# adaLN terms as VectorE dot products with outputs on partitions; the first scale on TensorE by tile pairs

## The chip, the cores and the metric

The kernel runs on one core of a Trainium2 chip. The metric is the device time of one execution in microseconds (us), the median of several. A core has TensorE (PE in the profile, its weight loads PEld), VectorE (DVE), ScalarE (ACT), GpSimd (POOL) and SyncE (SP, which here only issues transfers); each takes its instructions in the order in which they stand, and 16 DMA engines move the data. Data lies in SBUF or, for matmul results, in PSUM, on 128 partitions.

## The reference

One decoder block for 256 tokens of width 2048, all in fp32. The part that the change touches is the conditioning (adaLN): six vectors of 2048 numbers, each a product of the same vector with 2048 columns of a 2048 x 12288 matrix.

```python
c_act = jax.nn.silu(c)                                   # c: 1 x 2048
mod = (c_act @ w_ada[l] + b_ada[l])[:, None, :]          # 2048 x 12288: 100 MB
sh1, sc1, gt1, sh2, sc2, gt2 = jnp.split(mod, 6, axis=-1)
h = rms_norm(x, g_pre_mix[l]) * (1.0 + sc1) + sh1
z = h @ w_in[l]                                          # 2048 x 8000
...
mix = (g_a * o_a + g_b * o_b) @ w_o[l]                   # two attentions, gated
x = x + gt1 * rms_norm(mix, g_post_mix[l])
h = rms_norm(x, g_pre_ffn[l]) * (1.0 + sc2) + sh2
u = causal_dwconv(h @ w_up[l], conv_w[l], conv_b[l])
y = (jax.nn.silu(u[..., :D_FF]) * u[..., D_FF:]) @ w_down[l]
x = x + gt2 * rms_norm(y, g_post_ffn[l])
```

## The kernel before

Activations are kept transposed: a column of 128 channels stands on the partitions, the 256 tokens along the row. So a scale or shift is needed as one number per partition, in a tile of 128 x 16 (`s1`, `sh1`, `gt1`, `s2`, `sh2`, `gt2`).

Weights come as tiles of 128 x 1024 fp32 (512 KB) through SP's queue. For the large products each tile is split into a rounded high part (L116, ScalarE) and a low part (L117, VectorE), and TensorE multiplies in three terms (L129 to L131; L136 and L138 in the later stages). The adaLN matrix isn't split. Its 192 tiles go one of two ways:
- On TensorE (L234): the conditioning vector, padded to 32 columns (`cpad`), is the stationary operand, and the tile streams through. Four groups of columns use four strips of the array.
- On VectorE (L240 for the first tile, L242 for the others): `acc` gathers tile times the vector's number of that partition. At the end four matmuls with a matrix of ones sum `acc` over the partitions (L247).
Either way the result lies along a row, is copied to `rows` (L249, ScalarE) and turned onto the partitions by matmuls with the identity (L270, L300).

The first scale and shift are made together in six k-groups of 2, 2, 2, 2, 4 and 4 blocks of 128 channels (`early_gen`). `SHARE` sends every second tile of the last three groups to VectorE. While the first projection works on group k (stages z0 to z5, `early_z`), the tiles of group k+1 are issued in between; they lie in four buffers of their own (`raw2`), every second one of group 0 in the weights' ring. The later terms (`cols_gen`: gt1, s2, sh2 from z5 through attention and the output projection, gt2 in the up projection) run wholly on VectorE and share the weights' ring. A generator yields after each tile, and `pump` advances it at a rate per weight tile; a scheduler that keeps a timeline of its own then sets the final order of the instructions on each engine. The transfers stand in SP's queue in that order.

At the start, x is squared on ScalarE (L211), summed over the partitions by 16 matmuls with ones (L213), and the reciprocal root (L215, L216) scales x.

Stages on the trace, in us from the span's start: startup to 24.4, z0 to 56.5, z1 to 91, z2 to 115.5, z3 to 163, z4 to 219.5, z5 and attention to 650, output projection to 755, up projection to 980, the rest to 1503.8.

Of the kernel before, what the change touches and what calls it, by code (L numbers as in the profile page):

```python
# [24 lines left out]
SHARE = [99, 99, 99, 2, 2, 2]  # L25
# [18 lines left out]
def block_kernel(ctx: ExitStack, tc: tile.TileContext, a, out: bass.AP):  # L44
# [136 lines left out]
    ones = const.tile([P, P], F32, name="ones")  # L181
    pool.memset(ones, 1.0)
# [16 lines left out]
    cth = const.tile([P, KC], F32, name="cth")  # L199
# [7 lines left out]

    ps_ss = bank("tp")
    for k in range(0, KC, 2):
        sq = xp.tile([P, 512], F32, tag="sq", bufs=2, name="sq").rearrange("p (a b) -> p a b", a=2)  # L210
        act.activation(sq, xT[:, k:k + 2, :], AF.Square)  # L211
        for i in range(2):
            pe.matmul(ps_ss[:, :T], ones, sq[:, i, :], start=(k + i == 0), stop=(k + i == KC - 1))  # L213
# [5 lines left out]
    def ada_gen(src, width, rows, col, on_pe, share=10**9, spread=False):  # L219


        nj = KC // src.shape[0]
        w = 4 * width
        n = src.shape[0]
        acc = None
        ps = bank(on_pe) if on_pe else None
        for t in range(n):
            raw = load_bg(src[t], nj * w, spread and t % 2 == 1)
            for i in range(nj):
                j = t * nj + i  # L230
                if on_pe and t % share != share - 1:
                    for g in range(4):
                        o = i * w + g * width
                        pe.matmul(ps[32 * g:32 * g + 32, :width], cpad[:, j, :], raw[:, o:o + width],  # L234
                                  start=(j == 0), stop=(j == KC - 1 and share > n))
                    continue
                r = raw[:, i * w:i * w + w]
                if acc is None:
                    acc = const.tile([P, WT], F32, tag="acc", bufs=1, name="acc")
                    dve.tensor_scalar(acc[:, :w], r, csil[:, j:j + 1], None, op0=ALU.mult)  # L240
                else:
                    dve.scalar_tensor_tensor(acc[:, :w], r, csil[:, j:j + 1], acc[:, :w], op0=ALU.mult, op1=ALU.add)  # L242
            yield
# [12 lines left out]

    def early_gen(kg, k0, s):

        w = s * 64
        with ExitStack() as order:  # L260
            if kg:
                order.enter_context(tc.issue_after(split_ins[1].ins))
# [654 lines left out]
```

## Time and profile before

| | |
|---|---|
| time, median of 3 runs | 1502.75 us (1501.55 to 1503.86) |
| the profiled execution's own time | 1505.71 us |
| its span, first to last instruction | 1503.8 us |
| mean granted clock of TensorE | 0.988 |
| TensorE busy | 1452.7 us (97%) |
| VectorE busy | 1083.8 us (72%) |
| ScalarE busy | 775.6 us (52%) |
| GpSimd busy | 260.9 us (17%) |
| HBM read | 351.11 MB, 236 GB/s over the span |

The profile is one execution, some 0.2% longer than the median of the runs. An engine's busy time is a sum over stages that have different limits, so it says little of any one. A busy TensorE isn't TensorE at its peak: matmul ends are modelled, and what a run of small matmuls costs is better read from how far apart its neighbours start.

### The profile page before, as it was taken

The numbers are of one execution on the slowest core, as the hardware profiler recorded it, in microseconds if no ns is written. First come the engines' busy times: TensorE is split into PE (matmuls) and PEld (weight loads), VectorE is DVE, ScalarE is ACT, GpSimd is POOL, SyncE is SP. The second block draws the span as 40 slices with busy tenths as digits, with TensorE's granted clock in tenths as the row PEclk, the third lists the DMA queues.
The fourth block names the chain that finished last, engine by engine and source line by source line (L and its number), as shares of the span: only waits on it lengthen the run. The fifth ranks groups of instructions, "written<-read, shape, count | busy, mean of one in ns | idle before, by whom it ended". The sixth has DMA issues, their size and how long they took to land.

```text
span 1503.8 us, 24728 instructions
## 1 busy us (share of the span) xinstructions
PE 1452.7 (97%) x9506; PEld 1278.0 (85%) x9506; DVE 1083.8 (72%) x1488; ACT 775.6 (52%) x1223; POOL 260.9 (17%) x191
## 2 busy tenths in 40 slices
PE   7999999889999999999899989999999999999997
PEld 6988899789899998978788878888888888888886
DVE  3579868978887969767788777877767776444443
ACT  4534435545554655755655445655555555434442
POOL 0034315922413425300000000100000000000000
PEclk9999999999999999999899999999999999999999
DMA  9888868588687867659477777765555557555552
GB/s 373 312 313 323 311 233 266 180 272 271 201 298 235 301 228 259 202 201 388 178 243 251 239 253 266 251 209 190 187 190 189 189 190 242 193 195 190 191 193 99
DMA packets 101525, 356.96 MB, mean 237 GB/s; under 512 B 11760, under 2 KB 12208, under 8 KB 100896
## 3 DMA queue, kind: packets, MB, share of 16 engines
q1 hardware_dynamic: 99936, 350.82, 68.4%
q0 software_dynamic: 1472, 4.58, 1.2%
q8 instruction: 74, 1.21, 0.3%
q14 instruction: 43, 0.35, 0.1%
HBM read 351.11 MB, written 4.24 MB: 236 GB/s over the span
## 4 chain that ended last, share of the span: by engine, by line
PE 38%; DMA 10%; DVE 5%; ACT 1%; issue 1%; SPq 0%; DVEq 0%; ACTq 0%
PE bk_mm L136 8%; PE bk_sc L136 6%; DMA raw<-in_w_ada_dram 6%; PE bk_mm L138 4%; PE bk_sc L138 3%; PE bk_mm L144 3%; PE bk_sc L144 3%; PE bk_sc L146 3%; PE bk_mm L146 3%; PE bk_mm L145 3%; PE bk_sc L145 3%; DMA raw<-in_w_up_dram 2%; DVE acc L242 2%; DMA raw<-in_w_o_dram 2%; DVE wlo L117 2%
## 5 line engine op out<-in xcount | busy, mean ns | idle before, releaser
L117 DVE TENSOR_TENSOR wlo<-raw,whi 128x1024 fp32r<-128x1024 f32 (+3 forms) x472 | 594.3, 1266 | 282.8 <-ACT whi L116 280.7
L116 ACT CAST whi<-raw 128x1024 fp32r<-128x1024 f32 (+3 forms) x472 | 478.3, 1021 | 504.8 <-PE bk_mm L130 91.2
L129 PE MATMUL bk_mm<-h,whi 128*128 128x256 f32 x976 | 284.3, 292 | 0.5 <-DVE pair L376 0.5
L131 PE MATMUL bk_mm<-h,wlo 128*128 128x256 f32 x976 | 279.3, 287 | 0.0
L130 PE MATMUL bk_mm<-h,whi 128*128 128x256 f32 x976 | 279.1, 286 | 0.0
L136 PE MATMUL bk_mm<-h,whi 128*128 128x512 f32 x848 | 266.6, 396 | 1.2 <-ACT whi L116 1.2
L242 DVE SCALAR_TENSOR_TENSOR acc<-raw,csil,acc 128x1024 f32<-128x1024 f32 (+1 forms) x141 | 192.1, 1362 | 57.9 <-DMA raw<-in_w_ada_dram 57.3
L129 PEld LDWEIGHTS bk_mm<-h,whi 128*128 128x128 f32 x976 | 187.9, 193 | 16.0 <-issue 11.6
L138 PEld LDWEIGHTS bk_mm<-h,wlo 128*128 128x128 f32 x848 | 158.7, 188 | 44.8 <-DVE wlo L117 7.8
L130 PEld LDWEIGHTS bk_mm<-h,whi 128*128 128x128 f32 x976 | 188.3, 193 | 1.7 <-issue 1.7
L131 PEld LDWEIGHTS bk_mm<-h,wlo 128*128 128x128 f32 x976 | 187.8, 193 | 1.4 <-issue 1.3
L136 PE MATMUL bk_sc<-h,whi 128*128 128x512 f32 x560 | 177.1, 398 | 0.0
L138 PE MATMUL bk_mm<-h,wlo 128*128 128x256 f32 x848 | 167.4, 279 | 4.8 <-DVE wlo L117 4.8
L136 PEld LDWEIGHTS bk_mm<-h,whi 128*128 128x128 f32 x848 | 129.2, 189 | 1.9 <-ACT whi L116 1.4
L138 PEld LDWEIGHTS bk_sc<-h,wlo 128*128 128x128 f32 x560 | 105.4, 189 | 27.3 <-DVE wlo L117 2.6
L761 POOL TENSOR_TENSOR sa<-sa,u 128x512 f32<-128x512 f32 x22 | 33.4, 1520 | 472.8 <-DVE u L755 436.6
L138 PE MATMUL bk_sc<-h,wlo 128*128 128x256 f32 x560 | 110.6, 279 | 1.6 <-DVE wlo L117 1.6
L374 POOL TENSOR_TENSOR pair<-pair,part 128x512 f32<-128x512 f32 x35 | 64.5, 1843 | 190.2 <-ACT part L373 190.1
L136 PEld LDWEIGHTS bk_sc<-h,whi 128*128 128x128 f32 x560 | 85.7, 190 | 0.4 <-issue 0.4
L144 PE MATMUL bk_sc<-whi,g 128*128 128x512 f32 x176 | 68.6, 390 | 0.0
L144 PE MATMUL bk_mm<-whi,g 128*128 128x512 f32 x176 | 68.6, 390 | 0.0
L145 PE MATMUL bk_mm<-wlo,g 128*128 128x512 f32 x176 | 68.5, 389 | 0.0
(197 smaller groups left out, 2261.1 us busy)
## 6 DMA issues: line engine op xcount, KB each, us to landing
raw<-in_w_ada_dram SPq DMA_DIRECT2D x192, 512.0 KB, 5.1
raw<-in_w_up_dram SPq DMA_DIRECT2D x176, 512.0 KB, 4.6
raw<-in_w_in_dram SPq DMA_DIRECT2D x116, 512.0 KB, 5.2
raw<-in_w_down_dram SPq DMA_DIRECT2D x88, 512.0 KB, 4.5
raw<-in_w_o_dram SPq DMA_DIRECT2D x32, 512.0 KB, 5.7
raw<-in_w_uqn_dram SPq DMA_DIRECT2D x16, 384.0 KB, 4.0
bias<-trow POOLq DMA_DIRECT2D x16, 256.0 KB, 4.9
raw<-in_w_ukv_dram SPq DMA_DIRECT2D x16, 256.0 KB, 3.6
```

What stands on the lines that cost most here:

```text
L116: act.copy(hi[:, :n], raw[:, :n])
L117: dve.tensor_tensor(lo[:, :n], raw[:, :n], hi[:, :n].bitcast(F32), op=ALU.subtract)
L129: pe.matmul(o, wh, xh, start=start, stop=False)
L130: pe.matmul(o, wh, xl, start=False, stop=False)
L131: pe.matmul(o, wl, xh, start=False, stop=stop)
L136: pe.matmul(o, w[0], x[2], start=start and i == 0, stop=False)
L138: pe.matmul(o[:, :T], w[1], x[0], start=False, stop=stop and i == 1)
L144: pe.matmul(o, ch, wh, start=start, stop=False)
L145: pe.matmul(o, ch, wl, start=False, stop=False)
L146: pe.matmul(o, cl, wh, start=False, stop=stop)
L242: dve.scalar_tensor_tensor(acc[:, :w], r, csil[:, j:j + 1], acc[:, :w], op0=ALU.mult, op1=ALU.add)
L374: pool.tensor_tensor(pairs[i][:, :wd], pairs[i][:, :wd], part[:, :wd], op=ALU.add)
```

## The change

What it does, part by part:
- All later terms and the first shift become dot products on VectorE. The matrix is laid out so that an output column stands on a partition and half of the inputs (1024) along the row; `csb` holds the conditioning vector spread over all partitions. One instruction (`tensor_tensor_reduce`) multiplies a tile by half of `csb`, writes the products over the tile, and sums them into one column, starting from the bias or from the first half's sum. L240, L242, L247, L249, L300 and L302 fall away for these terms. There are 160 such instructions: 128 for the later terms, 32 for the shift (4 each for k-groups 0 to 3, 8 each for 4 and 5). Before, there were 152 on VectorE: 144 at 1024 elements, 8 at 512.
- The first scale is all on TensorE, half the columns of before (64 wide instead of 128 in a tile of a 2-block group, 128 instead of 256 in a 4-block group). For groups 1 to 5 two tiles are gathered, and their matmuls are issued together, the newer tile first. `SHARE` is gone.
- `csb` is made at the start by 16 transposes and four copies on ScalarE. The squares of x are added up on VectorE (seven adds), and two matmuls with ones remain; `ones` becomes a broadcast of one column; the root's table is touched early.
- `pT` has two buffers instead of three; four empty yields of gt2 are dropped; both halves of group 0's shift go into the weights' ring.

The core of the diff (the host's new layout and some small lines are left out):

```diff
@@ block_kernel, start
-    ones = const.tile([P, P], F32, name="ones")
-    pool.memset(ones, 1.0)
+    one = const.tile([P, 1], F32, name="one")
+    pool.memset(one, 1.0)
+    ones = one.broadcast_to([P, P])
...
+    csb = const.tile([P, D], F32, name="csb")
+    for k in range(0, KC, 4):
+        b = bank("mm")
+        for j in range(4):
+            turn_pe(b[:, j * P:j * P + P], csil[:, k + j:k + j + 1].broadcast_to([P, P]))
+        act.copy(csb[:, k * P:(k + 4) * P], b)
+    ssx = xp.tile([P, 512], F32, name="ssx")
+    for k in range(0, KC, 2):
+        sq = ssx if k == 0 else xp.tile([P, 512], F32, tag="sq", bufs=2, name="sq")
+        act.activation(sq.rearrange("p (a b) -> p a b", a=2), xT[:, k:k + 2, :], AF.Square)
+        if k:
+            dve.tensor_tensor(ssx, ssx, sq, op=ALU.add)
     ps_ss = bank("tp")
-    for k in range(0, KC, 2):
-        sq = xp.tile([P, 512], F32, tag="sq", bufs=2, name="sq").rearrange("p (a b) -> p a b", a=2)
-        act.activation(sq, xT[:, k:k + 2, :], AF.Square)
-        for i in range(2):
-            pe.matmul(ps_ss[:, :T], ones, sq[:, i, :], start=(k + i == 0), stop=(k + i == KC - 1))
+    for i in range(2):
+        pe.matmul(ps_ss[:, :T], ones, ssx[:, i * T:i * T + T], start=i == 0, stop=i == 1)
...
-    def ada_gen(src, width, rows, col, on_pe, share=10**9, spread=False):
...
+    def dot(src, t, dst, cols, init, spread=False):
+
+
+        cc, kh = t // 2, t % 2
+        raw = load_bg(src[t], WT, spread)
+        to = half if kh == 0 else dst[:, cols + cc:cols + cc + 1]
+        dve.tensor_tensor_reduce(raw, raw, csb[:, kh * WT:kh * WT + WT], 1.0,
+                                 bada[:, init + cc:init + cc + 1] if kh == 0 else half,
+                                 op0=ALU.mult, op1=ALU.add, accum_out=to)
...
     def early_gen(kg, k0, s):
...
-        yield from ada_gen(a["w_ada1"][kg], w, rows, 0, "sc", SHARE[kg], kg == 0)
...
+        ps = bank("sc")
+        held = []
+        for t in range(2 * s):
+            held.append((t, load_bg(a["w_ada1s"][kg][t], WT)))
+            if kg == 0 or len(held) == 2:
+                start = t < 2 if kg else t == 0
+                for u, raw in reversed(held):
+                    for i in range(nj):
+                        for g in range(4):
+                            o = i * w + g * width
+                            pe.matmul(ps[32 * g:32 * g + 32, :width], cpad[:, u * nj + i, :], raw[:, o:o + width],
+                                      start=start and i == 0, stop=t == 2 * s - 1 and i == nj - 1 and u == held[0][0])
+                    start = False
+                held = []
+            yield
+            dot(a["w_ada1h"][kg], t, sh1, k0, k0, kg == 0)
+            yield
+        act.copy(rows[:, :width], ps[:, :width])
...
     def cols_gen(which, dst, bofs, gofs):
 
-        for half in range(2):
-            yield from ada_gen(a["w_ada2"][which][half], T, rows, half * T, None)
-
-        for _ in range(4 if which == 3 else 0):
+        for t in range(2 * KC):
+            dot(a["w_ada2"][which], t, dst, 0, bofs)
             yield
-        ps = bank("tp")
-        for b in range(4):
-            pe.matmul(ps[:, 4 * b:4 * b + 4], rows[:, b * P:(b + 1) * P], ident[:, 0:P:32], start=True, stop=True)
...
-            pT = at.tile([P, 384], F32, tag="pT", bufs=3, name="pT")
+            pT = at.tile([P, 384], F32, tag="pT", bufs=2, name="pT")
```

How the order moves is shown at three places. On TensorE in stage z1, before: tiles of group 2 (`raw_793`, `raw_809`) stand between three-term matmuls (L129 to L131); L234 is the adaLN matmul on TensorE.

```order
L129 MATMUL bk_mm<-h,whi 128x256
L130 MATMUL bk_mm<-h,whi 128x256
L131 MATMUL bk_mm<-h,wlo 128x256
L234 MATMUL bk_sc<-raw_793,cpad 32x128 x6
L234 MATMUL bk_sc<-raw_809,cpad 32x128 x8
L129 MATMUL bk_mm<-h,whi 128x256
L130 MATMUL bk_mm<-h,whi 128x256
L131 MATMUL bk_mm<-h,wlo 128x256
L129 MATMUL bk_mm<-h,whi 128x256
```

At the same place of the changed kernel (its lines are one lower; L268 is the adaLN matmul):

```order
L128 MATMUL bk_mm<-h,whi 128x256
L129 MATMUL bk_mm<-h,whi 128x256
L130 MATMUL bk_mm<-h,wlo 128x256
L268 MATMUL bk_sc<-raw_807,cpad 32x64 x6
L268 MATMUL bk_sc<-raw_732,cpad 32x64 x16
L128 MATMUL bk_mm<-h,whi 128x256
L129 MATMUL bk_mm<-h,whi 128x256
L130 MATMUL bk_mm<-h,wlo 128x256
L128 MATMUL bk_mm<-h,whi 128x256
```

Where two tiles of 128 columns stood (part of one, and another), a pair stands: 22 matmuls of 64 columns.

On TensorE in the attention stretch, before, at the end of a term: L247 are the ones-matmuls, L300 the transposes of `rows`; L578 and L583 are attention's matmuls with the values.

```order
L578 MATMUL bk_o<-pT,vt 128x256
L578 MATMUL bk_o<-pT,vt 128x128
L583 MATMUL bk_o<-pT,pair 64x256 x2
L583 MATMUL bk_o<-pT,pair 64x128 x2
L247 MATMUL bk_tp<-acc,ones 32x256 x4
L300 MATMUL bk_tp<-c_ident,rows 128x4 x2
L131 MATMUL bk_mm<-h,wlo 128x256
L129 MATMUL bk_mm<-h,whi 128x256
```

The changed kernel, behind attention's matmuls with the values (L581 there) at this place:

```order
L129 MATMUL bk_mm<-h,whi 128x256
L581 MATMUL bk_o<-pT,pair 64x256
L581 MATMUL bk_o<-pT,pair 64x128 x2
L130 MATMUL bk_mm<-h,wlo 128x256
L128 MATMUL bk_mm<-h,whi 128x256
L129 MATMUL bk_mm<-h,whi 128x256
```

The six small matmuls of the term's end are gone, and the three-term matmuls follow directly.

On VectorE in the startup, before: L216 is the reciprocal root, L264 scales x by it, L275 to L277 finish scale and shift, L282 applies them, and L159 and L117 are splits.

```order
L216 RECIPROCAL rstd<-rstd 128x256
L264 TENSOR_TENSOR xT<-xT,rstd 128x256 x2
L275 SCALAR_TENSOR_TENSOR s_145<-bk_tp,c_b_adaT 128x2
L277 TENSOR_TENSOR sh_146<-bk_tp,c_b_adaT 128x2
L276 TENSOR_TENSOR s_145<-s_145,c_gcol 128x2
L282 TENSOR_SCALAR xT<-xT,s_145,sh_146 128x256 x2
L159 TENSOR_TENSOR h<-xT,h 128x2x256
L117 TENSOR_TENSOR wlo<-raw,whi 128x1024
```

The changed kernel, from the reciprocal root (L228) on; each dot stands as two rows (the operation, then the read of its accumulator, both called ISA), `sh_167` is the first shift and `s_166` the first scale, and L256, L283, L284 and L288 stand for L264, L275, L276 and L282:

```order
L228 RECIPROCAL rstd<-rstd 128x256
L237 ISA raw,sh_167<-raw,csb,half 128x1024
L237 ISA sh_167 128x1
L256 TENSOR_TENSOR xT<-xT,rstd 128x256 x2
L237 ISA raw,half<-raw,csb,c_b_adaT 128x1024
L237 ISA half 128x1
L237 ISA raw,sh_167<-raw,csb,half 128x1024
L237 ISA sh_167 128x1
L283 SCALAR_TENSOR_TENSOR s_166<-bk_tp,c_b_adaT 128x2
L284 TENSOR_TENSOR s_166<-s_166,c_gcol 128x2
L288 TENSOR_SCALAR xT<-xT,s_166,sh_167 128x256 x2
```

Three of the four dots of group 0 stand between the reciprocal and the scale's two small operations (the first stands ahead of the reciprocal); the shift's own small operation is gone.

## Rows read from the trace of the kernel before

**Rows 1.** Windows: length; PE, PEld, DVE, ACT, POOL busy us; PEclk, DMA share, GB/s.
```profile
24.40:56.50 32.10, 32.10 (x319) 28.91 (x316) 15.29 (x19) 19.97 (x30) 0.00 (x0) 0.95 0.99 377
56.50:219.50 163.00, 163.00 (x1474) 146.31 (x1475) 127.53 (x162) 66.16 (x86) 47.77 (x26) 1.00 0.84 295
219.50:650.00 430.50, 408.82 (x3182) 385.46 (x3181) 363.53 (x588) 240.56 (x480) 174.58 (x131) 0.98 0.75 246
755.00:980.00 225.00, 217.50 (x1245) 185.96 (x1244) 183.62 (x235) 122.60 (x177) 16.34 (x10) 1.00 0.77 253
```

**Rows 2.** Groups by line, 24.4 to 219.5 us, TensorE's adaLN matmuls.
```profile
L234 PE MATMUL bk_sc<-raw,cpad 128*32 128x128 f32 x308 | 15.1, 279 | 0.0
L234 PE MATMUL bk_sc<-raw,cpad 128*32 128x256 f32 x128 | 12.6, 391 | 0.0
L247 PE MATMUL bk_sc<-acc,ones x24: 272/379/403, 109.0 to 213.3; 128*32 128x256 f32 x16, 128*32 128x128 f32 x8
```

**Rows 3.** Groups by line and shape, whole span: busy us, mean ns, idle before.
```profile
L242 DVE SCALAR_TENSOR_TENSOR acc<-raw,csil,acc 128x1024 f32<-128x1024 f32 x134 | 186.5, 1391 | 57.9 <-DMA raw<-in_w_ada_dram 57.3
L240 DVE TENSOR_SCALAR acc<-raw,csil 128x1024 f32<-128x1024 f32 x10 | 7.9, 792 | 2.9 <-PE bk_tp L247 2.3 <-DMA raw<-in_w_ada_dram 0.5
```

**Rows 4.** VectorE's timeline in the attention stretch: start us, us, instruction.
```profile
518.39 1.28 DVE L242 SCALAR_TENSOR_TENSOR acc<-raw,csil,acc 128x1024 f32<-128x1024 f32 x1
519.59 0.34 DVE L555 CUSTOM_DVE_ANT_0 sm<-bk_sc,bias,c_sink 128x128 f32<-128x128 f32 x1
519.86 0.48 DVE L555 CUSTOM_DVE_ANT_0 sm<-bk_sc,bias,c_sink 128x256 f32<-128x256 f32 x1
520.26 0.08 DVE L555 DVE_READ_ACCUMULATOR2_ANT mx<- 128x1 f32 x1
```

**Rows 5.** TensorE's timeline at three places in z1 and z3.
```profile
68.42 0.28 PE L131 MATMUL bk_mm<-h,wlo 128*128 128x256 f32 x1
68.63 1.07 PE L234 MATMUL bk_sc<-raw,cpad 128*32 128x128 f32 x28
...
69.85 0.28 PE L130 MATMUL bk_mm<-h,whi 128*128 128x256 f32 x1
...
76.63 0.28 PE L131 MATMUL bk_mm<-h,wlo 128*128 128x256 f32 x1
76.84 0.64 PE L234 MATMUL bk_sc<-raw,cpad 128*32 128x128 f32 x16
...
77.64 0.28 PE L130 MATMUL bk_mm<-h,whi 128*128 128x256 f32 x1
77.76 0.28 PE L131 MATMUL bk_mm<-h,wlo 128*128 128x256 f32 x1
...
123.63 0.28 PE L131 MATMUL bk_mm<-h,wlo 128*128 128x256 f32 x1
123.84 0.64 PE L234 MATMUL bk_sc<-raw,cpad 128*32 128x256 f32 x8
...
124.63 0.28 PE L130 MATMUL bk_mm<-h,whi 128*128 128x256 f32 x1
```

**Rows 6.** Chain of work that ended last, up projection, in order of time.
```profile
852.68 0.57 PE bk_tp L247 x8
...
879.44 1.30 DVE acc L242
880.75 5.54 DMA raw<-in_w_ada_dram
...
975.21 0.79 PE bk_tp L300 x8
```

**Rows 7.** Timeline of TensorE and VectorE at the end of the startup.
```profile
20.35 0.64 PE L234 MATMUL bk_sc<-raw,cpad 128*32 128x128 f32 x16 [0.64 <-DMA raw<-in_w_ada_dram]
...
21.80 0.16 DVE L275 SCALAR_TENSOR_TENSOR s<-bk_tp,c_b_adaT 128x2 f32<-128x2 f32 x1 [0.20 <-PE bk_tp L270]
...
22.19 0.74 DVE L282 TENSOR_SCALAR xT<-xT,s,sh 128x256 f32<-128x256 f32 x2
```

## What the trace leads to

> **What bounds the kernel now.** I read the busy table by stage first [rows 1], because a share over the whole span would mix stages with different limits. From 24.4 to 56.5 us TensorE shows no gap and the DMA engines are 99% busy at 377 GB/s: two limits at once. From 56.5 to 219.5 us, where the first projection runs on the later k-groups, TensorE is again busy for all 163.00 us, VectorE for 127.53, the DMA for 84%: an instruction taken off TensorE is time. In the attention stretch (219.5 to 650) TensorE is busy 408.82 of 430.50 us and VectorE 363.53: TensorE mostly, with 21.7 us of waits for others. In the up projection (755 to 980) TensorE is busy 217.50 of 225 us, and the chain that ended last runs partly through a loop of its own [rows 6]: an adaLN tile lands (5.54 us), VectorE folds it in (1.30 us), and only then does the buffer come free for the next. After 980 us no adaLN work is left, and the change touches nothing.
>
> So I price three things: matmul runs taken off TensorE, VectorE's instruction per adaLN tile, and the waits of a half's end. A TensorE run is priced by what it does to the regular matmuls around it [rows 5]. Three-term matmuls follow each other at 0.12 us (77.64 to 77.76). From the L131 ahead of a run of 16 records (76.63) to the second matmul behind it (77.64) are 1.01 us instead of 0.24: price 0.77. For 28 records it is 69.85 − 68.42 − 0.24 = 1.19; for 8 records of 256 columns 124.63 − 123.63 − 0.24 = 0.76. From the first two, (1.19 − 0.77)/12 = 0.035 us a record of 128 columns and 0.77 − 16 × 0.035 = 0.21 for every run, however short; a 256-column record is (0.76 − 0.21)/8 = 0.069.
>
> **The dot product on VectorE.** No row shows it at 128x1024 with both sources in SBUF. The nearest are the softmax's fused operations, which also end in an accumulator [rows 4]: 128 elements step 0.27 us (519.59 to 519.86), 256 step 0.40 (519.86 to 520.26), so 0.13/128 = 1.0 ns an element; 1024 elements make 0.27 + 896 × 0.00104 = 1.20, and the same with rounding 1.17 to 1.25. The scale-and-add that it replaces steps 1.20 (518.39 to 519.59). The two are equal; the accumulator read lies under the next instruction. Only where a multiply alone stood (mean 0.79 us against 1.39 [rows 3], the first tile of each half or group) does a dot cost some 0.5 us more, 11 times. Total VectorE work: 12 dots are new (four in the startup, four each for k-groups 1 and 2), 15 us, in stretches where VectorE has 17 us (z0) and 35 us (z1 to z4) free [rows 1]. Cost 0; if that cover were gone, 1.2 us each.
>
> [...] The rows here speak for full rate as far as they reach: the scale-and-add has two fp32 SBUF sources and steps at 1.20 us per 1024, but has no accumulator; the softmax rows have an accumulator, but one of their sources is in PSUM. No row has both. [...]
>
> **Startup.** The last adaLN tile lands at 20.35, and its matmuls, a row copy, two transposes and three small operations stand between it and the scaling of x at 22.19 [rows 7]. Afterwards the last tile is a shift tile: a dot, 20.35 + 1.25 = 21.6, and two small operations of about 0.15, 21.9. The scale's own path starts one tile earlier and is done by then. The 16 transposes for the spread c, the copies and the seven adds lie in a TensorE and VectorE that wait for the DMA. −0.3, bounds −1 to +1, since z0 behind it is held by the DMA.
>
> **z1 to z4.** Before, from 24.4 to 219.5, 308 records of 128 columns, 128 of 256 [rows 2] in 46 runs (counted in the order), and 24 records with the ones (8 of 128 columns, 16 of 256) in 3 more: 49 × 0.21 + 308 × 0.035 + 128 × 0.069 + 8 × 0.035 + 16 × 0.069 = 10.3 + 10.8 + 8.8 + 0.3 + 1.1 = 31.3 us. After: half the columns only, in pairs, 28 runs in the order, 192 matmuls of 64 columns and 128 of 128; the trace writes two records for a matmul, so 384 and 256. A 64-column record isn't in the trace: 0.018 if it goes by columns, 0.035 if it costs what 128 cost; between, 0.026. 28 × 0.21 + 384 × 0.026 + 256 × 0.035 = 5.9 + 10.0 + 9.0 = 24.9. Gain 6.4, of which z0 (9 runs before, 3 after, 128 records at either time) has 6 × 0.21 + 128 × 0.009 = 2.4; there the DMA is full, so it counts nothing. −4.0; bounds: −7 (64 columns by columns, all of z0) and −1 (64 columns as dear as 128, and a part eaten by the transfers). The order shown for z1 has this: two runs of tiles become one whole run of 22 matmuls with half the columns.
>
> **Attention.** Five half-ends with their four ones-matmuls go (5 × 0.76 = 3.8) and two ends with transposes (16 records; eight took 0.79 in the chain [rows 6], so 1.6): 5.4 us off TensorE. The row copies on ScalarE and VectorE's wait for a free accumulator go too; VectorE gets 5 × 0.5 more. Since TensorE waits in 5% of this stretch for others, and what is removed may only bring it sooner to such a wait, I take half: −2.7, bounds −6 and 0. w_o gets one half-end less, 0 to −0.76: taken as 0, since no row here shows that TensorE sets the time there.
>
> **Up projection.** Two half-ends (such as that at 852.68, 0.57 in the chain, 0.76 with the turn) and eight transposes at 975.21 (0.79) lie on the chain: 2.3 us. The first is followed by the loop, which takes its start from DMA and VectorE, so its gain is lost: −1.6. The loop's own period changes only by dot against scale-and-add (1.30, below 0.05) and by the read: 32 × 0.08 [rows 4] = 2.6 worse if the freed buffer waits for the read as well. Bounds −3 to +1.5.
>
> **Sum.** −0.3 − 4.0 − 2.7 − 1.6 = −8.6 us, 0.6%. The profiled execution took 1505.71 with a span of 1503.8; the median of the runs is 1502.75, 0.2% lower, and the difference is taken off that: 1494.15, so **1494.0 us**. Its own range from the bounds above, not all at one end: 1488 to 1500.
>
> **Rivals.**
> A. [...] 4%.
>
> B. Slower, through the pairs. TensorE takes its instructions in order, and a pair's run starts with the newer tile; if that hasn't landed, all three-term matmuls queued behind it wait. A tile takes 1.39 us at 377 GB/s [rows 1]. With 14 pairs, the other gains are used up from a mean wait of 8.6/14 = 0.61 us; a whole tile each is 19.5 − 8.6 = +10.9, about 1513. Held tiles also keep two of four background buffers longer, and the transfers behind them on SP's queue wait. For it: z1 to z4 have the DMA at 84%, with little margin. Against: before, TensorE shows no gap at all there. 10%.
>
> C. Nothing: the time won on TensorE in z1 to z4 comes back as a wait for weights, and that of the later stages in the loop and in VectorE, whose waits for adaLN tiles (57.3 us in all [rows 3]) show that these stages often go by arrivals. 1500 to 1505. 15%.
>
> D. A larger gain than 15 us, when attention gives all 5.4 and the 64-column records go by columns with their stalls: 7%. The forecast keeps 64%.
>
> A difference of 0.2%, 3 us, is about what runs of this kernel can tell from none. Faster 0.64 + 0.07 = 0.71, same 0.15 (C), slower 0.14 (A, B). The range 1487 to 1506 leaves out D's larger part, A and most of B.
>
> **What would show it.** Right: dots of 1.2 to 1.3 us with the next instruction 1.2 after; in 24.4 to 219 TensorE without gap and z1 to z4 some 4 us shorter; fused runs of about 0.21 + 0.026 a record; no rows of ones-matmuls after 219 us; attention 2 to 3 us shorter; the up loop with the same period. Wrong: dots above 2 us (A); TensorE waiting for adaLN tiles ahead of a pair (B); equal stage lengths with new waits for weights (C); 64-column records at 0.035 or above, which alone takes 3.5 us off the gain.

## The result: slower by 0.7%

| | before | after |
|---|---|---|
| time, median of 5 runs | 1502.75 us (1500.90 to 1506.24) | 1513.75 us (1511.28 to 1515.97) |
| ratio, 95% interval | | 1.0071 (1.0053 to 1.0088) |
| profiled execution, its span | 1505.71, 1503.8 us | 1511.28, 1509.5 us |

The forecast was 1494.0 with a range of 1487 to 1506. It was wrong, and in its sign. The two profiled executions lie at opposite ends of their runs (before's near the longest, after's is the shortest), so they stand 5.6 us apart where the medians stand 11.0.

Where the time goes is read by equal progress: in both traces I take the start of the same record of the split products (8096 records of matmuls on `whi` and `wlo`, in order of time) and subtract. By these records, z2 ends and z4 starts in before's trace at some 119 and 169 us, which is later than the list of stages has it. The first column is before's time in us, the others are differences to it; the kernels from the third on are the experiments below.

| record | before | after | late_only | early_only | before_in_order | in_order_2 |
|---|---|---|---|---|---|---|
| 600th, end of z2 | 119.4 | -9.2 | +2.9 | -9.4 | +0.8 | -9.5 |
| 950th, start of z4 | 170.1 | +1.1 | +3.5 | +0.1 | +0.8 | +0.1 |
| 1325th, start of z5 | 220.5 | +0.2 | +4.2 | 0.0 | +0.8 | -0.4 |
| 4224th, end of output projection | 749.0 | +16.4 | +16.2 | +5.8 | -5.0 | -10.4 |
| 5464th, end of up projection | 980.1 | +5.8 | +8.7 | -2.4 | -15.2 | -23.6 |

After wins 9.2 us up to the end of z2 and has lost them soon after z4 starts; it loses 16.2 from z5 to the end of the output projection; it wins 10.6 in the up projection. One profile of each kernel stands behind a column, and executions of one kernel differ by some 6 us (the runs of before, 1500.9 to 1506.2), so a stage's few us prove nothing alone: early_only has before's order of the late operations, and still stands 5.8 us behind before from z5 to the output projection's end and 8.2 ahead in the up projection.

**Up to z4.** Windows of after (length; PE, PEld, DVE, ACT, POOL busy; PEclk, DMA share, GB/s), for [rows 1]:

```profile
0.00:165.00 165.00, 146.05 (x1649) 136.13 (x1649) 133.25 (x182) 80.26 (x114) 35.02 (x30) 1.00 0.91 327
56.50:219.50 163.00, 155.31 (x1625) 147.29 (x1624) 136.08 (x178) 64.01 (x84) 41.52 (x26) 0.98 0.85 294
110.00:170.00 60.00, 52.58 (x544) 48.25 (x544) 54.54 (x74) 23.19 (x31) 16.78 (x11) 0.97 0.90 320
219.50:666.00 446.50, 408.58 (x3123) 385.67 (x3122) 370.58 (x680) 240.66 (x475) 165.82 (x131) 0.97 0.74 238
771.00:986.00 215.00, 213.86 (x1222) 185.00 (x1221) 180.66 (x264) 120.34 (x173) 18.46 (x10) 1.00 0.80 264
```

The first window of before, and its z3:

```profile
0.00:165.00 165.00, 155.90 (x1500) 136.52 (x1501) 107.84 (x146) 76.68 (x106) 39.27 (x29) 0.99 0.90 328
119.00:170.00 51.00, 51.00 (x435) 45.01 (x435) 46.20 (x61) 22.52 (x29) 20.80 (x11) 1.00 0.91 326
```

From 110 to 170 us, where the lead is lost, VectorE is busy 54.54 of 60 us and TensorE 52.58. In before's z3 VectorE was busy 46.20 of 51.00 us: 4.8 us were free there, and the change puts 8.3 us more into it. By 165 us TensorE has been busy 9.85 us less and VectorE 25.4 us more (some 5.2 and 8.8 of that in the startup); the DMA has moved the same (327 against 328 GB/s).

The lead goes in two parts. Within z3 it shrinks from 9.2 us to 5.7 at the 920th record (before's 165 us). The other 5.9 us go in one stop, between the 920th record and the 940th, where z4 starts. TensorE's and VectorE's timelines of after there, and the window behind the stop (reads of the accumulator are left out):

```profile
163.55 1.08 PE L268 MATMUL bk_sc<-raw,cpad 128*32 128x128 f32 x32 [1.92 <-DMA raw<-in_w_ada1s_dram]
164.56 0.62 PE L128 MATMUL bk_mm<-h,whi 128*128 128x256 f32 x3
168.70 0.58 PE L129 MATMUL bk_mm<-h,whi 128*128 128x256 f32 x1 [3.52 <-DVE h L158]
169.08 0.41 PE L130 MATMUL bk_mm<-h,wlo 128*128 128x256 f32 x1
169.29 0.41 PE L128 MATMUL bk_mm<-h,whi 128*128 128x256 f32 x1
...
162.17 1.38 DVE L288 TENSOR_SCALAR xT<-xT,s,sh 128x256 f32<-128x256 f32 x4
163.46 1.22 DVE L116 TENSOR_TENSOR wlo<-raw,whi 128x1024 fp32r<-128x1024 f32 x1
164.59 2.30 DVE L237 CUSTOM_DVE_ANT_0 raw<-raw,csb,c_b_adaT 128x1024 f32<-128x1024 f32 x1
166.83 1.22 DVE L116 TENSOR_TENSOR wlo<-raw,whi 128x1024 fp32r<-128x1024 f32 x1
167.96 1.28 DVE L158 TENSOR_TENSOR h<-xT,h 128x512 fp32r<-128x512 f32 x2
...
168.70:172.70 4.00, 4.00 (x18) 4.00 (x19) 3.09 (x7) 0.00 (x0) 0.00 (x0) 0.50 1.01 393
```

TensorE first waits 1.92 us for a tile of a pair. Then it waits 3.52 us for group 4's split: between the scaled x of group 4 (done at 163.5) and its split (167.96) stand two weight splits and a dot for group 5. Behind that TensorE runs its matmuls 0.21 us apart (169.08 to 169.29) where 0.12 is usual [rows 5], at a granted clock of 0.50 for 4.00 us.

The price list of the prediction nearly held. TensorE's timeline in z1 of after, two runs of 64-column records:

```profile
77.40 0.28 PE L130 MATMUL bk_mm<-h,wlo 128*128 128x256 f32 x1
77.61 0.43 PE L268 MATMUL bk_sc<-raw,cpad 128*32 128x64 f32 x16
...
78.19 0.28 PE L129 MATMUL bk_mm<-h,whi 128*128 128x256 f32 x1
...
78.66 0.28 PE L130 MATMUL bk_mm<-h,wlo 128*128 128x256 f32 x1
78.87 0.75 PE L268 MATMUL bk_sc<-raw,cpad 128*32 128x64 f32 x36
...
79.78 0.28 PE L129 MATMUL bk_mm<-h,whi 128*128 128x256 f32 x1
```

16 records cost 0.79 - 0.24 = 0.55, 36 cost 1.12 - 0.24 = 0.88: 0.0165 a record, by columns, as the lower of my two bounds had it (0.018), and 0.29 a run instead of 0.21.

**The dot.** Lines of after, and VectorE's timeline at one dot:

```profile
L237 DVE CUSTOM_DVE_ANT_0 raw<-raw,csb,c_b_adaT x80: 1261/1284/2392, 13.7 to 947.1; 128x1024 f32<-128x1024 f32 x80
...
500.09 1.27 DVE L237 CUSTOM_DVE_ANT_0 raw<-raw,csb,half 128x1024 f32<-128x1024 f32 x1
501.30 0.08 DVE L237 DVE_READ_ACCUMULATOR2_ANT s<- 128x1 f32 x1
501.30 0.85 DVE L564 TENSOR_SCALAR sm<-sm,den 128x128 f32<-128x128 f32 x1
```

The next instruction starts 1.21 us later; forecast 1.20. This dot took 1.27 us, not above 2 (A).

**Attention.** Waits of after from 219.5 us to the end of attention (us in total, times, longest), then those of before:

```profile
DVE raw L237 <- DMA raw<-in_w_ada_dram: 68.5, 42, 4.6
PE bk_sc L548 <- DVE mx L553: 19.9, 6, 4.9
```

```profile
DVE acc L242 <- DMA raw<-in_w_ada_dram: 27.4, 23, 2.6
PE bk_sc L550 <- DVE mx L555: 10.5, 5, 4.0
```

VectorE stands 68.5 us in front of adaLN tiles that haven't landed, against 27.4, and TensorE waits 19.9 instead of 10.5 for the softmax, which VectorE does. All of TensorE's waits from 219.5 to 655 us add up to 37.9 us against 21.5: 16.4 more, the size of the loss. Besides the softmax it is the weight splits, for which TensorE waits 9.5 us instead of 3.6. One such place of after, VectorE's timeline (without the reads of the accumulator), TensorE's, and windows around it:

```profile
478.55 1.29 DVE L237 CUSTOM_DVE_ANT_0 raw<-raw,csb,c_b_adaT 128x1024 f32<-128x1024 f32 x1 [4.65 <-DMA raw<-in_w_ada_dram]
...
486.85 2.32 DVE L237 CUSTOM_DVE_ANT_0 raw<-raw,csb,c_b_adaT 128x1024 f32<-128x1024 f32 x1
489.09 3.42 DVE L116 TENSOR_TENSOR wlo<-raw,whi 128x1024 fp32r<-128x1024 f32 x2
492.44 1.27 DVE L237 CUSTOM_DVE_ANT_0 raw<-raw,csb,half 128x1024 f32<-128x1024 f32 x1
493.64 0.34 DVE L553 CUSTOM_DVE_ANT_0 sm<-bk_sc,c_cmask,c_sink 128x128 f32<-128x128 f32 x1
...
494.45 1.22 PE L548 MATMUL bk_sc<-kss,qs 128*128 128x128 f32 x4 [4.64 <-DVE mx L553]
495.47 0.41 PE L129 MATMUL bk_mm<-h,whi 128*128 128x256 f32 x1
495.68 0.41 PE L130 MATMUL bk_mm<-h,wlo 128*128 128x256 f32 x1
...
489.50:494.40 4.90, 0.31 (x3) 0.10 (x1) 4.90 (x9) 1.15 (x3) 0.80 (x1) 0.92 0.73 219
494.40:499.00 4.60, 4.55 (x22) 4.55 (x22) 4.60 (x10) 2.82 (x10) 3.08 (x2) 0.50 0.75 230
```

VectorE stands 4.65 us in front of the tile that lands at 478.4. From there to the softmax (L553) it has no gap but one of 0.20 us, and the two dots and two splits of the last 7 us stand ahead of it; so the late start reaches the softmax. TensorE waits 4.64 us for it, and from 494.4 to 499 us the granted clock is 0.50: matmuls stand 0.21 us apart (495.47 to 495.68) instead of 0.12. At that pace these 4.6 us lose some 2.0 more (an estimate, 4.6 × 0.09/0.21).

What differs is VectorE's order. I count it as a place: at how many weight tiles of SP's order a late tile's operation stands too early (by splits on VectorE that belong to tiles loaded before it, but stand behind it). Over the 84 late tiles from z5 to the end of attention the mean is 0.27 early before (32 of them exactly in order) and 1.60 early after (15 and 47 of them two or more early). The transfers stand in the same order in both. In after's trace a dot in its order (11 of them) doesn't wait for its tile; one place early it waits 0.25 us on average (26), two early 1.15 (33), three early 1.7 (14).

### The profile page after: what moved, and what is told of

Its sections match the earlier page's. It is cut to its first block, busy times and chain, and to the rows that moved or that the text cites. A ratio compares the mean times of both kernels' runs of the same rounds, so it can differ in the third digit from the quotient of the medians.

```text
span 1509.5 us, 24945 instructions
## 1 busy us (share of the span) xinstructions
PE 1433.6 (95%) x9570; PEld 1275.8 (85%) x9570; DVE 1112.6 (74%) x1653; ACT 777.0 (51%) x1220; POOL 248.8 (16%) x191
## 4 chain that ended last, share of the span: by engine, by line
PE 73%; DMA 10%; DVE 10%; issue 4%; ACT 2%; POOL 1%; SPq 0%; DVEq 0%; ACTq 0%; POOLq 0%
PE bk_mm L135 12%; PE bk_sc L135 8%; DMA raw<-in_w_ada_dram 8%; PE bk_mm L137 6%; PE bk_mm L128 6%; PE bk_mm L129 5%; PE bk_mm L130 5%; DVE wlo L116 5%; PE bk_mm L144 4%; PE bk_mm L145 4%; PE bk_mm L143 4%; PE bk_sc L137 4%; PE bk_sc L144 3%; PE bk_sc L145 3%; PE bk_sc L143 3%
## 5 line engine op out<-in xcount | busy, mean ns | idle before, releaser
L129 PE MATMUL bk_mm<-h,whi 128*128 128x256 f32 x976 | 281.3, 289 | 3.5 <-DVE h L158 3.5
L129 PEld LDWEIGHTS bk_mm<-h,whi 128*128 128x128 f32 x976 | 190.0, 195 | 5.5 <-DVE h L158 3.7
L237 DVE CUSTOM_DVE_ANT_0 raw<-raw,csb,c_b_adaT 128x1024 f32<-128x1024 f32 x80 | 113.9, 1424 | 50.5 <-DMA raw<-in_w_ada_dram 45.9
L237 DVE CUSTOM_DVE_ANT_0 raw<-raw,csb,half 128x1024 f32<-128x1024 f32 x80 | 111.0, 1387 | 52.8 <-DMA raw<-in_w_ada_dram 47.0
L372 POOL TENSOR_TENSOR pair<-pair,part 128x512 f32<-128x512 f32 x35 | 59.1, 1688 | 196.7 <-ACT part L371 196.6
```

The source lines that it names most:

```text
L129: pe.matmul(o, wh, xl, start=False, stop=False)
L237: dve.tensor_tensor_reduce(raw, raw, csb[:, kh * WT:kh * WT + WT], 1.0, bada[:, init + cc:init + cc + 1] if kh == 0 else half, op0=ALU.mul ...
L372: pool.tensor_tensor(pairs[i][:, :wd], pairs[i][:, :wd], part[:, :wd], op=ALU.add)
```

## The experiments

Theory O: that place costs the time, whatever operation stands there. Rivals: E (the early part shifts everything behind it), P (the dot itself, or `pT` with two buffers, costs it), D (a dot costs it where it stands early, a scale-and-add in that place doesn't).

**1. Each half alone: late_only, early_only.** The first is before with `cols_gen`, `dot` and `csb` of the change (and two `pT` buffers, since `csb` takes the room), the second is the change with before's `ada_gen` and `cols_gen` for the later terms.

> Only the later terms (gt1, s2, sh2, gt2) are dot products; startup, first scale and first shift stay as before; pT has two buffers, as in the changed kernel, since the spread c takes the room. VectorE's order from z5 on is that of the changed kernel. Theory O (the order of VectorE: dots stand ahead of weight splits that were loaded before them, so VectorE stands in front of tiles that haven't landed and the softmax behind it is late): attention and output projection lose some 16 us and the up projection wins some 10, as in the changed kernel: about 1508, within 1504 to 1514. Rival E (the loss comes from the early part, whose shorter z0 to z2 shift everything behind it): about 1493 to 1498.

> Only the startup, the first shift and the first scale are changed (dots, pairs, squares); the later terms stay scale-and-add with ones-matmuls, pT has three buffers. Theory O: z0 to z2 win some 9 us and z3 gives them back while it waits for its VectorE work, so z4 begins within 2 us of before; attention as before; total 1503, within 1500 to 1506. Rival E: attention is slower too, 1512 or above. By the sum of the prediction (z1 to z4 and startup only): 1498.5.

late_only: 1515.42 us, ratio 1.0086 (1.0073 to 1.0099), 1.4 us above my range. early_only: 1503.12, 1.0001 (0.9989 to 1.0013). The loss comes with the later terms, and E falls. The early part, for which I forecast 4.3 us, is worth nothing: it wins 9.4 by the end of z2 and has nothing left at z4 (0.1 behind).

**2. The late dots' place: in_order, in_order_2, one_later.** In the changed kernel:

```diff
-                dve.tensor_tensor(lo[:, :n], raw[:, :n], hi[:, :n].bitcast(F32), op=ALU.subtract)
+                W["lo"] = dve.tensor_tensor(lo[:, :n], raw[:, :n], hi[:, :n].bitcast(F32), op=ALU.subtract)
...
-        dve.tensor_tensor_reduce(raw, raw, csb[:, kh * WT:kh * WT + WT], 1.0,
+        with ExitStack() as order:
+            if inorder:
+                order.enter_context(tc.issue_after(W["lo"].ins))
+            dve.tensor_tensor_reduce(raw, raw, csb[:, kh * WT:kh * WT + WT], 1.0,
...
-            dot(a["w_ada2"][which], t, dst, 0, bofs)
+            dot(a["w_ada2"][which], t, dst, 0, bofs, inorder=True)
```

`issue_after` sets the order on the engine: in in_order_2 none of the 84 late dots stands early. The scheduler then orders the other engines anew.

In one_later the dot is kept back (`pend`) until the next weight tile's split is written, and stands behind that:

```diff
+                lo_ins = dve.tensor_tensor(lo[:, :n], raw[:, :n], hi[:, :n].bitcast(F32), op=ALU.subtract)
+                flush(lo_ins)
...
+            pend.append(go)
```

> The changed kernel, but every dot of a later term is ordered behind the split (wlo) of the weight tile that was loaded just before its own tile, so VectorE takes tiles in the order in which they were loaded. Theory O: VectorE's wait for adaLN tiles in attention falls from 68 us to 35 or less, the 16 us there are mostly won back and the up projection keeps its 10: 1494 to 1500. Rival P (the second pT buffer, or the dot itself, costs the time, not its place): 1511 to 1515, as the changed kernel.

> The changed kernel, but every dot of a later term is ordered behind the split of the weight tile that was loaded after its own tile: one place later than in the kernel above. Theory O: VectorE hardly waits for adaLN tiles (below 10 us in attention), but their buffers of the ring come free later and the weights' transfers start later: between 1492 and 1506, and no better than the kernel above by more than 4 us. In the up projection the loop of one buffer gets a split longer, which may cost 5 to 15 us there. Rival P: 1511 or above.

> The kernel with late dots in the order of loading once more, since its profiled execution was one in which TensorE ran at about a fifth of its pace from end to end, and shows no stage. Its timed runs were 1482.33 to 1482.72. Theory O: 1482.5 again; VectorE's wait for adaLN tiles between z5 and the end of attention below 35 us (68 us in the changed kernel), TensorE's waits for the softmax on VectorE below 10 us (20 us), and that stretch shorter than before's by some 8 us or more; z0 to z4 as in the changed kernel; the up projection keeps its gain of some 10.

in_order: 1482.64 us, 0.9862 (0.9848 to 0.9877), and again 1481.84, 0.9842 (0.9823 to 0.9861): 32 us faster than the changed kernel by an order alone, more than I expected. Rival P falls: the dots and the two `pT` buffers are still there. (Its first profile shows an execution of 7908.94 us, told of at the end, so that the stages come from the second.) VectorE no longer waits for adaLN tiles in attention at all; it waits 35.4 us for ScalarE's high parts instead of 3.3, and TensorE's waits there fall from 37.9 to 17.8 us.

The edit isn't as narrow as it looks. Against the changed kernel, only 2 of 696 transfers stand elsewhere in in_order_2, but so do some 500 of TensorE's 9570 records and some 140 of ScalarE's 1100. No run holds the other engines' order, so what their part in the 32 us is stays open.

one_later: 1516.13, 1.0086 (1.0074 to 1.0098), above my range. There, too, VectorE doesn't wait for adaLN tiles, and it is 4.9 us ahead of before at the end of the output projection (in_order_2: 10.4). But it loses 17 us in the up projection: an adaLN tile then lies some 5 us in its buffer before its dot (1 us in in_order_2), and a tile takes some 6.8 us against 5.8. The chain that ended last runs there through the weight tiles' transfers and splits, not through the dots as in [rows 6].

**3. The same for before: before_in_order.** Its scale-and-adds (L240, L242) in the same way:

```diff
+                with ExitStack() as order:
+                    if not on_pe:
+                        order.enter_context(tc.issue_after(W["lo"].ins))
```

> The kernel before, with its scale-and-adds of the later terms ordered behind the split of the weight tile loaded just before, as the late dots in the kernel above; nothing else changed. Theory O in its strong form (the place on VectorE is all that counts): it wins what the dots won by it in attention, some 8 to 12 us, but not the up projection's 10, since the half's end with its ones-matmuls stays: 1491 to 1496. Theory O in its weak form (the order only undoes a loss that before didn't have; before was in order at 38% of its late tiles and one early at 29%): 1500 to 1505.

1489.84 us, 0.9902 (0.9886 to 0.9919), 14.6 us under before in the same set of runs. The weak form falls, and the total is the strong form's, but not its stages: by the traces 5.8 us come from z5 to the end of the output projection (8 to 12 expected in attention) and 10.2 in the up projection, where I expected none and where before's own profile may be slow by most of it (early_only). At nearly equal places the change then wins: 1481.84 against 1489.84 in the same set of runs, 8.0 us, where I had forecast 8.6.

**4. Early places: before_one_early, before_as_early, dots_one_early.** The first two contain no dot. A split is held back behind the scale-and-add of the tile loaded after it:

```diff
+                if ltm["on"]:
+                    pump()
+                with ExitStack() as order:
+                    if ltm["acc"] is not None:
+                        order.enter_context(tc.issue_after(ltm["acc"].ins))
+                    dve.tensor_tensor(lo[:, :n], raw[:, :n], hi[:, :n].bitcast(F32), op=ALU.subtract)
```

Here `ltm["acc"]` is the scale-and-add that `pump` has just issued. In before_one_early this goes on from z5 to the end of the up projection.

In before_as_early all splits of a group of tiles are held so, up to the end of attention. dots_one_early pins each late dot of the changed kernel between the two splits ahead of and behind the place one early.

> The kernel before, no dot in it, but from z5 on every split is ordered behind the scale-and-add of the adaLN tile loaded next after its weight tile, so the scale-and-adds stand one place early, nearly as the dots of the changed kernel do (mean 1.15 places early against 1.6 there and 0.27 before). Theory O (the place on VectorE costs the time, whatever the operation): VectorE's wait for adaLN tiles in attention rises from 28 us to 55 or more and the kernel is slower, 1510 to 1520. Rival P (a dot in that place costs more than a scale-and-add): 1500 to 1506.

> The kernel before, no dot in it; from z5 to the end of attention the splits of a group of weight tiles are ordered behind the scale-and-adds of the adaLN tiles that were loaded with and behind them, so the scale-and-adds stand as early on VectorE as the dots of the changed kernel (mean 1.61 places, against 1.60). Theory O, place alone: VectorE's wait for adaLN tiles in attention 55 us or more, and attention 10 to 18 us longer than before's, total 1511 to 1522. Theory D (a dot early costs, a scale-and-add in that place doesn't): attention within 5 us of before's, total 1499 to 1508.

> The changed kernel, every late dot from z5 to the end of attention pinned exactly one place early: behind the split of the weight tile loaded two before its own, ahead of the split of the one loaded just before it; as in the kernel before with its scale-and-adds one place early, which took 1504.0. Theory O, place alone, with the 8 us that the change wins at equal places (in order: 1489.8 against 1481.8): 1496, within 1492 to 1501. Theory D: 1505 to 1516.

before_one_early: 1504.02, 0.9997 (0.9977 to 1.0017), a miss: VectorE's wait for tile or `acc` rose only from 29.7 to 41.0 us, and the time not at all. before_as_early: 1516.54, 1.0092 (1.0072 to 1.0112). With scale-and-adds as early as the dots, the kernel before is as slow as the changed one, though TensorE waits elsewhere: 13.3 us for weight splits and 1.8 for the softmax. dots_one_early: 1485.80, 0.9887 (0.9869 to 0.9905), faster than I expected. Theory D falls in both. VectorE's waits in attention of before_as_early, before_one_early and dots_one_early:

```profile
DVE acc L255 <- DMA raw<-in_w_ada_dram: 50.9, 34, 3.0
DVE acc L253 <- PE bk_tp L260: 11.3, 4, 4.2
```

```profile
DVE acc L251 <- DMA raw<-in_w_ada_dram: 28.3, 28, 2.1
DVE acc L249 <- PE bk_tp L256: 12.7, 3, 5.7
```

```profile
DVE raw L250 <- DMA raw<-in_w_ada_dram: 24.4, 25, 2.4
```

The table adds how many of the 84 late tiles stand two or more places early, and the time from the 1325th record to the 4224th (start of z5 to the end of the output projection) in each profile:

| kernel | mean place | two or more early | VectorE's wait for tile or `acc`, us | z5 to output projection, us | median, us |
|---|---|---|---|---|---|
| before_as_early | 1.61 early | 48 | 62.2 | 541.1 | 1516.54 |
| after | 1.60 early | 47 | 68.5 | 544.8 | 1513.75 |
| before_one_early | 1.15 early | 10 | 41.0 | 522.9 | 1504.02 |
| dots_one_early | 1.02 early | 1 | 24.4 | 516.5 | 1485.80 |
| before | 0.27 early | 15 | 29.7 | 528.6 | 1502.75 |
| before_in_order | 0.43 late | 0 | 2.3 | 522.8 | 1489.84 |
| in_order_2 | in order | 0 | none | 518.6 | 1481.84 |

For either operation, 60 us of waiting is the slow end and none the fast one. In between neither the mean place nor the wait decides: before and dots_one_early wait nearly as long and are 17 us apart, of which the change explains 8. What orders the stretch is the third column: up to 10 tiles two or more early it takes 516 to 523 us, with 15 it takes 529 (early_only: 534), with 47 or 48 some 541 to 545 (late_only: 541). By this, one place early costs nothing that these runs can tell, and two or three cost the time. That is a reading of profiles at hand, not a forecast that was tested, and a stage of one kernel moves by some 6 us. before_one_early is no faster than before in total because it wins nothing in the up projection (231.4 us against before's 231.1 and 220.9 in before_in_order). Where the scale-and-adds stand early they also wait for `acc` (12.7 and 11.3 us), since the next half can't begin until TensorE has summed the last; the dots have no such wait.

**5. What z3 gives back: short_dots, all_in_order, no_pairs, split_first, half_tiles, half_both**, all on in_order's kernel; half_both is half_tiles and short_dots together. short_dots leaves three quarters of the shift's sum out, half_tiles half of the first scale's columns. Their edits, the core of each, in this order:

```diff
-            dot(a["w_ada1h"][kg], t, sh1, k0, k0, kg == 0)
+            dot(a["w_ada1h"][kg], t, sh1, k0, k0, kg == 0, n=256)
...
+            dot(a["w_ada1h"][kg], t, sh1, k0, k0, kg == 0, inorder=kg > 0)
...
-            if kg == 0 or len(held) == 2:
+            if True:
...
+        behind = split_ins[1] if kg else None
+                order.enter_context(tc.issue_after(behind.ins))
...
+            nw = WT // 2 if kg else WT
+            held.append((t, load_bg(a["w_ada1s"][kg][t][:, :nw], nw)))
+                            o = (i * w + g * width) % nw
```

> The kernel with late dots in the order of loading, but the 32 dots of the first shift read only 256 of their 1024 elements (the shift's sum is cut to a quarter; all transfers stay): some 0.8 us less of VectorE each, 24 of them in z0 to z3 or so. Theory V (VectorE became the limit in z2 and z3, which is why the 9 us won by TensorE until then are lost again): z4 begins 6 to 12 us earlier and the total is 1472 to 1478. Rival T (the adaLN tiles' arrival, by the DMA and the held buffers, sets the start of z4): z4 begins within 3 us of the same, total 1480 to 1484.

> The kernel with late dots in the order of loading, and the dots of the first shift for k-groups 1 to 5 as well behind the split of the weight tile loaded just before. If VectorE's stand in front of shift tiles (10 us between 100 and 225 in the changed kernel) is what costs z3: 1474 to 1479. If VectorE is short of time as such (theory V) or the tiles' arrival decides (T): within 3 us of 1482.5.

> The kernel with late dots in the order of loading, but each tile of the first scale is multiplied by itself, not in pairs: 14 runs on TensorE more, 14 x 0.21 = 3 us, and no tile is held for another. If held tiles delay the transfers (rival B of the prediction) the last tiles of k-group 4 land earlier and z4 begins earlier: 1474 to 1480. If the pairs only save runs and TensorE isn't the limit until z3's end: z0 to z2 lose up to 2 us, z4 begins within 1.5 us of the same, 1480 to 1484.

> The kernel with late dots in the order of loading, and the shift dots of a k-group ordered behind the split of the former group's activations, so that in z3 the dot for k-group 5 (2.3 us, and a weight split) no longer stands between the scaled x of group 4 and its split, for which TensorE waits 4 us. If that wait and the lower clock behind it are part of what z3 gives back: z4 begins 2 to 5 us earlier, 1477 to 1480. If the arrival of group 4's tiles decides alone: within 1.5 us of 1482.

> The kernel with late dots in the order of loading, but of each tile of the first scale for k-groups 1 to 5 only the first half of the columns is loaded, and the matmuls read that half twice (the first scale is wrong, the work on every engine stays): 24 tiles bring 256 KB instead of 512, of which some 5 MB of the 54 MB that arrive by 165 us. Theory T (the arrival of data sets z4's start): z4 begins 4 us or more earlier, up to 12; total 1470 to 1478. Theory V alone (VectorE's time): z4 begins within 1.5 us of the same, 1480 to 1484.

> The same with the half tiles, and also the shift's dots cut to 256 of 1024 elements, which alone moved z4's start by 4.5 us. If arrival and VectorE's time each hold z3 back: z4 begins 8 us or more earlier than with the order alone, all that z0 to z2 had won, 1468 to 1475. If one of them alone decides: as the better of the two runs, 1474 to 1479.

| kernel | 600th record | start of z4 | start of z5 | median, us |
|---|---|---|---|---|
| in_order_2 | -9.5 | +0.1 | -0.4 | 1481.84 |
| short_dots | -9.1 | -4.4 | -4.2 | 1478.22 |
| all_in_order | -8.1 | +1.1 | +0.2 | 1483.07 |
| no_pairs | -5.3 | -2.1 | -2.2 | 1480.56 |
| split_first | -8.2 | -0.6 | 0.0 | 1482.59 |
| half_tiles | -1.9 | +3.7 | -0.9 | 1481.58 |
| half_both | -4.6 | -0.4 | -3.2 | 1480.78 |

VectorE's time is a part: shorter dots bring z4 4.5 us forward, between the two forecasts. They keep the lead through z3 (9.8 us at the 920th record, 6.7 in in_order_2) and lose 4.5 in the stop at the start of z4, where TensorE still waits. all_in_order changes nothing: VectorE's stands in front of shift tiles aren't it. The pairs win 4 us by the end of z2; without them z4 starts 2.2 us earlier, and TensorE's wait there is 1.2 us. split_first changes nothing in the total, but it doesn't test the stop: two weight splits take the dot's place, and TensorE waits 4.1 us as before. Arrival by bytes gets no support: in half_tiles 305 instead of 327 GB/s come in by 165 us, and z4 starts later, not earlier. But with other tile sizes the scheduler also placed z1 and z2 otherwise, so the run isn't a clean one, and half_both missed both its forecasts. So the other half of the 9 us goes in TensorE's stop at the start of z4; what would take the stop away stays open. Of the six only short_dots differs from in_order_2 by more than 2 us: 3.6, with ranges that just touch.

## Why the prediction was wrong

- **Attention** is the step that failed: -2.7 us forecast (with 0 for the output projection), +16.2 measured. It priced what is taken off TensorE and put on VectorE, each in its old place. The change moved the late operations on VectorE from 0.27 to 1.60 places early, 47 instead of 15 of 84 tiles two or more early. That place costs some 14 us where no dot is involved (before_as_early, experiment 4), and without it the same dots win (in_order, experiment 2). The scheduler's order of the other engines changes along with it, and its share isn't separated. The move of places shows in the orders of both kernels without a run; I had read them only at the ends of the terms. In rival C I had read VectorE's 57.3 us of waits [rows 3] as time that swallows gains, not as a cost that a new order can double.
- **z1 to z4**: 4.0 forecast, nothing measured. The prices of runs were nearly right (a run 0.29 instead of 0.21, 64 columns cheaper than taken). That an instruction off a busy TensorE is time was wrong: TensorE was busy all along [rows 1], but where the lead is lost VectorE is busier than TensorE. The dots weren't free: I had set 12 new ones against 35 us of free VectorE in z1 to z4, but before's z3 had only 4.8 us free, and the change needs 8.3 there. short_dots, which cuts three quarters of each, gets 4.5 of the 9 us back. Cover read from one window of 163 us isn't cover in each stage of it. The other half goes in the stop at the start of z4, and its cause is open.
- **The dot's time**: right, 1.21 against 1.20. The dot has two fp32 sources in SBUF and an accumulator, and the 112 dots during which GpSimd is idle took 1.19 to 1.29 us. No run shows dots above 2 us throughout (A, which had 4% of the chances): in after's trace 15 of 160 took 2.07 to 2.39 us, all of them while GpSimd worked.
- **Up projection**: a gain, with 1.6 forecast. After is 10.6 us faster there, but early_only, whose up projection is before's, is 8.2 faster than before's profile too, so most of it is the spread between executions. At equal places (in_order_2 against before_in_order, from the 4224th record to the 5464th) it is 13.2 against 10.2: 3.0.
- **Startup**: within 0.6 us of no change in all profiles with the early part; forecast -0.3.
- **Rival B**: the slower sign and its size (1513) were there, by another mechanism. TensorE's wait for a pair's tile is 1.9 us in all up to z5, and without the pairs the kernel is within its runs' spread (no_pairs, 1480.56 against 1481.84).
- **The sum** of 8.6 fits what the change is worth at equal places, 8.0, but by luck, not by its terms. In the profiles of in_order_2 and before_in_order it is worth 1.2 us up to the start of z5 (where 4.3 were forecast), 4.2 from there to the end of the output projection (2.7 forecast) and 3.0 in the up projection (1.6 forecast): the early part was forecast too large and the others too small.

## What to carry to other kernels

Where a scheduler orders the instructions, a change of operation is a change of order: before pricing it, compare on each in-order engine where every operation that waits for a transfer stands against the order of the transfers. An operation that stands ahead of work whose data landed earlier makes that work late, here mostly from two places on, and the order alone was worth 15 us before the change and 32 after it; the best kernel of the study is the changed one with its late dots in the order of loading, 1482 us, 1.5% faster than before. Work taken off a busy engine won no time here where a second one was nearly as full: in before's z3 TensorE was busy for all 51.00 us and VectorE for 46.20. Read the cover stage by stage.

## What the runs showed of the hardware

- In the 4.6 us behind a wait of 4.64 us (494.4 to 499) TensorE's granted clock was 0.50, and in the 4.0 us behind the wait of 3.52 us ahead of 168.70 it was 0.50 too, with steps of 0.21 us instead of 0.12 in both. By these steps the two stretches lost some 2.0 and 1.7 us (an estimate), together somewhat under half of the two waits. Whether it was the waits that lowered the clock, no run tests.
- Of after's 160 dots the 112 without GpSimd at work took 1.19 to 1.29 us. Of the 48 others 21 took 1.26 to 1.29 and 27 took 1.54 to 2.39: that at 486.85 took 2.32, with GpSimd busy from 483.68 to 490.30, that at 492.44, with GpSimd idle, 1.27.
- One of the executions of in_order took 7908.94 us (its span 7907.2 us) at a mean granted clock of 1.00; its other three runs and the four of in_order_2, the same kernel, lie between 1478.84 and 1483.37. The cause isn't known.
